# Fourier mixing by halves and mirror images, convolution taps that read PSUM, and an earlier conversion of w_out, in a hybrid Fourier and Mamba-2 block

## The chip, the cores and the metric

The kernel runs on one core of a Trainium2 chip. The metric is the device time of one execution in microseconds (us). The engines are named as in the profile: PE is the matrix engine, PEld its weight load, DVE the vector engine, ACT the scalar engine, POOL the GpSimd engine, and SP the engine that only issues DMA transfers. PE writes its results to PSUM, which PE, DVE and ACT can reach; everything else lies in SBUF.

## The reference, cut to what matters

One layer: 2048 latent tokens of 1024 features and 256 context tokens pass a modulated norm, one input projection, a Fourier part and a bidirectional state-space scan, an output projection, and a feed-forward network. What the change touches is the part between input and output projection:

```python
def conv_rows(u, w, bias, rows, row_len):            # rows of 64 tokens; D_CONV = 7
    up = jnp.pad(u.reshape(b, rows, row_len, ch), ((0, 0), (0, 0), (half, half), (0, 0)))
    out = bias
    for k in range(D_CONV):
        out = out + up[:, :, k:k + row_len, :] * w[:, k]
    return out.reshape(b, L, ch)

def fourier_mix(u):                                  # 256 features = 4 groups of 64; 2048 tokens
    ug = u.reshape(b, L, N_FGROUPS, FGROUP_DIM).astype(jnp.float32)
    yf = jnp.fft.fft2(ug, axes=(1, 3), norm='ortho').real
    return yf.reshape(b, L, F_WIDTH).astype(u.dtype)

def mixer_inputs(h, w_in, conv_w, conv_b, rows, row_len, full):
    p = h @ w_in
    u_f, z, rest = p[..., :F_WIDTH], p[..., F_WIDTH:XBC_OFF], p[..., XBC_OFF:]
    xbc = jax.nn.silu(conv_rows(rest[..., :CONV_DIM], conv_w, conv_b, rows, row_len))
    ...

def mixer_output(u_f, z, xs, y, d_skip, g_ssd, w_out):
    ...
    y = rms_norm(y * jax.nn.silu(z), g_ssd)
    return jnp.concatenate([fourier_mix(u_f), y], axis=-1) @ w_out
```

The Fourier part needs only the real part of a two-dimensional transform of real input. Such a transform has a symmetry: the value at (token frequency l, feature frequency f) is the complex conjugate of that at (-l, -f).

## The kernel before, in words

**Stages.** The first 760 us or so hold the input projection with everything that hangs on it: the convolutions, the step sizes ("dt"), the forward scan, the Fourier part, and the split of weights. After it come the output stage, chunk by chunk, and the feed-forward network. All matmuls of the projection are done in three passes of a 32-bit format (hi x hi, hi x lo, lo x hi), so each weight block is split into `hi` and `lo` (`wparts`, on ACT and on POOL or DVE), and so is w_out (`load_wo`, ACT and DVE).

**Blocks.** The projection is a list `blocks` of 128 output columns each, for three sections of tokens: 0 and 1 are the halves of the latent tokens (1024 each), 2 is the context (256). Kinds: z (gate), u (Fourier input), x, B, C (convolved), and dt. A block of a latent section is 48 matmuls of 512 columns (`project`, 2 halves x 8 x 3), into a PSUM tile "mm" of two banks, of which there are two. A further PSUM pair "y" serves dt, the first Fourier stage and the output stage; two single banks "a" serve transposes, the scan, the second Fourier stage and other small work. Those are all eight banks.

**Convolution.** `conv` copies the finished block from PSUM to a tile `u` (ACT), forms the middle tap with the bias (ACT, from PSUM, into `acc`), and then runs six taps on DVE, each a multiply-add of `u`, shifted, into `acc`. `to_tokens` then transposes the block through PE in two groups of four into "a" banks, and ACT copies these out.

**Fourier.** `fourier_steps` runs once section 1's u blocks are done, for one half of the 256 features after the other (`fb`). For each, the first stage multiplies 16 token groups with the matrix `dft1` (cosines and sines of all 64 feature frequencies, two groups of 64 features side by side, 256 columns); a radix-4 `butterfly` (POOL one subtraction, DVE one addition and six halves and quarters) and complex turns (two ACT copies, two DVE operations each) follow, four times (`j`); then, for four `p`, another butterfly and the second stage: 8 matmuls with constants `kf` that are loaded from memory each time, and one ACT copy into `fo`. So there are 16 butterflies. `fo` is written to memory at the end of each half.

**What sets the order.** PE, DVE, ACT and POOL execute in the order in which the program writes their instructions. That order comes from a planner, `Pace`: each side job (a block's convolution, the Fourier step, the scan, the modulation rows `ada_steps`) is a generator, a chain with a time at which its next step is due; after each matmul step of a block, `pace.due()` issues the steps whose time has come by the planner's own costs (a DVE multiply-add costs 0.06 us + n/960, for instance). `spare()` holds a Fourier step back while the planner believes DVE to be more than 1.2 us behind. `pace.drain(chains)` issues the rest of a chain at once. `finish_block` drains the chains of all earlier blocks but the last before a new one goes on. DMA loads are issued from SP (`dma`), most stores from ACT (`put`); a queue issues in order, and a load that must wait for its buffer holds up those behind it.

**The end of the stage.** At the last block but two the chains of all blocks but z, and the scan, are drained; at the last block the Fourier step, the first chunk's front, and the conversion of the first half of w_out (`late`) are; the conversion of the second half runs beside that last block. `late_steps` starts the first conversion when the Fourier step is done:

```python
        def late_steps():
            fourier_load(pend[0])
            decay_loads(pend[0])
            late.append(pace.start(load_wo(0, "B"), 4.0))
```

The lines that name the operations: in the profile nearly every instruction carries the planner's helper line L140, so groups are told apart by their tiles: `acc<-u,convw,acc` is a tap, `u<-mm` the copy from PSUM, `y<-kc,actB` the first Fourier stage, `a<-kf,gg` the second, `gg` and `actB` the butterflies and turns, `a<-ident,acc` a transpose, `h<-h,a` a step of the scan's state, `dtp` the dt chain, `actB<-wo` a conversion of w_out.

Of the kernel before, what the change touches and what calls it, by code (L numbers as in the profile page):

```python
# [21 lines left out]
P = 128  # L22
# [10 lines left out]
HD = 64  # L33
# [8 lines left out]
def shape_constants():  # L42
# [8 lines left out]
    dft1 = np.zeros((2, HD, 2, 2, HD))  # L51
    f = np.arange(HD)
    ang = 2 * np.pi * ((f[:, None] * f[None, :]) % HD) / HD
# [4 lines left out]
    dft1 = dft1.reshape(P, 4 * HD).astype(np.float32)  # L58
# [10 lines left out]
class Pace:  # L69
# [43 lines left out]
    def drain(self, *chains):  # L113

        self.forced += 1
        for chain in chains:
            while not chain.done:
# [44 lines left out]
def fourier_ssd_block(ctx, tc, a):  # L162
# [87 lines left out]
    kc = cq.tile([P, 2 * P + 24 + 256], F32, name="kc")  # L250
# [152 lines left out]
    hdec = cq.tile([P, NCH + 2, 24], F32, name="hdec")  # L403
    acs_d = [scratch(f"acsd{h}", [8 * 24, P]) for h in range(2)]
# [14 lines left out]
    def project(w, acts, half=None, beside=None):  # L419
        ps = mm()  # L420
# [13 lines left out]
    def dt_section(acts, sec):  # L434
# [3 lines left out]
        ps = pair()  # L438
# [9 lines left out]
        S.copy(sb[:, 0 : nch * P], ps[0:48].rearrange("p a b -> p (a b)")[:, 0 : nch * P])  # L448

# [70 lines left out]
    def conv(ps, n, row, j, res):  # L520
        long = n == HALF
        u = g_.tile([P, n], F32, tag="u" if long else "l_cT", name="u")
        convs.append(u)
        S.copy(u, ps[:, 0:n])
        acc = g_.tile([P, n], F32, tag="acc" if long else "sc", name="acc")
        S.activation(acc, ps[:, 0:n], AF.Identity, bias=convb[:, j : j + 1], scale=convw[:, j, 3:4])
        yield
        ur = u.rearrange("p (r c) -> p r c", c=row)
        ar = acc.rearrange("p (r c) -> p r c", c=row)
        for k in (2, 4, 1, 5, 0, 6):  # L530
# [3 lines left out]
            while convs[0] is not u:  # L534
                yield 0.1
# [3 lines left out]
        convs.pop(0)  # L539
        S.activation(acc, acc, AF.Silu)  # L540
# [15 lines left out]
    def column_block(kind, j, sec, ps):  # L556
# [4 lines left out]
        if kind == "x":  # L561
            yield from conv(ps, n, row, j, res)
            yield from to_tokens(res[0], n, xtok_d[sec], j)
        elif kind == "B":
            yield from conv(ps, n, row, XB + j, res)
# [3 lines left out]
        elif kind == "C":  # L569
            yield from conv(ps, n, row, XB + BB + j, res)  # L570
            put(cT_d[sec][j], res[0])
        elif kind == "z":
            sz = g_.tile([P, HALF], F32, tag="tok", name="sz")
            S.activation(sz, ps, AF.Silu)
            put(szT_d[sec][j], sz)
            last_sz[:] = [sz]
        elif kind == "u":
            uf = g_.tile([P, HALF], F32, tag="tok", name="uf")
            S.copy(uf, ps)
            put(ufT_d[sec][j], uf)  # L580
# [89 lines left out]
    def butterfly(dst, src, pool):  # L670
# [6 lines left out]
        V.tensor_tensor(dst(0), s[:, 0, :], s[:, 1, :], op=ALU.add)  # L677
        V.tensor_tensor(dst(2), s[:, 0, :], s[:, 1, :], op=ALU.subtract)
        re, im = slice(0, P), slice(P, 2 * P)
        V.tensor_tensor(dst(1)[:, re], d[:, 0, re], d[:, 1, im], op=ALU.add)  # L680
        V.tensor_tensor(dst(1)[:, im], d[:, 0, im], d[:, 1, re], op=ALU.subtract)
        V.tensor_tensor(dst(3)[:, re], d[:, 0, re], d[:, 1, im], op=ALU.subtract)
        V.tensor_tensor(dst(3)[:, im], d[:, 0, im], d[:, 1, re], op=ALU.add)
        yield

    def fourier_steps():
        tt = act("B", F32, (P, 4, 4, 256))
        wk = act("B", F32, (P, 4, 4, 256))
        for fb in range(2):
            uf = wk[:, 0:2].rearrange("p a b c -> p (a b c)")  # L690
            for h in range(2):
                dma(uf[:, h * HALF : (h + 1) * HALF], ufT_d[h][fb])
            yield 10.0
            for j in range(4):
                ps = pair()
                for m in range(4):
                    n2 = 4 * m + j
                    T.matmul(ps[:, m // 2, (m % 2) * 256 : (m % 2 + 1) * 256], uf[:, n2 * P : (n2 + 1) * P], dft1,
                             start=True, stop=True)
                va = wk[:, 2]  # L700
                S.copy(va.rearrange("p (a b) c -> p a (b c)", a=2), ps)
                yield
                yield from butterfly(lambda p: tt[:, p, j, :], va, wk[:, 3])
                for ps_ in ((1, 2), (3,)) if j else ():
                    turned = []
                    for i, p in enumerate(ps_):
                        th = -2 * math.pi * j * p / 16
                        xx, tm, tn = tt[:, p, j, :], wk[:, 3, 2 * i, :], wk[:, 3, 2 * i + 1, :]
                        S.activation(tm, xx, AF.Copy, scale=0.0 if j * p == 4 else math.cos(th))
                        S.copy(tn, xx)  # L710
                        turned.append((xx, tm, tn, math.sin(th)))
                    yield from spare()
                    for xx, tm, tn, ci in turned:
                        V.scalar_tensor_tensor(xx[:, 0:P], tn[:, P : 2 * P], -ci, tm[:, 0:P], ALU.mult, ALU.add)
                        V.scalar_tensor_tensor(xx[:, P : 2 * P], tn[:, 0:P], ci, tm[:, P : 2 * P], ALU.mult, ALU.add)
                    yield
            fo = wk[:, 0:2].rearrange("p a b c -> p (a b c)")
            fov = fo.rearrange("p (l q r) -> p r q l", q=4, r=4)
            for p in range(4):
                kf = g_.tile([P, 4, 2, P], F32, tag="xt", name="kf", bufs=4)  # L720
                dma(kf, a["k_f"][:, p])
                gg = g_.tile([P, 4, 256], F32, tag="xt", name="gg", bufs=4)
                yield from butterfly(lambda q: gg[:, q, :], tt[:, p], wk[:, 3])
                yield 0.3
                ps = bank()
                for q in range(4):
                    for i in range(2):
                        T.matmul(ps[:, q * P : (q + 1) * P], gg[:, q, i * P : (i + 1) * P], kf[:, q, i, :],
                                 start=i == 0, stop=i == 1)
                S.copy(fov[:, p], ps.rearrange("p (q l) -> p q l", q=4))  # L730
                yield
            put(fT_d[fb], fo)
# [566 lines left out]
    def load_wo(n, slot):  # L1299

        wo_hi.append(act(slot))
        wo_lo.append(act(slot))
        for kp in range(KD // 2):
            raw = wo_raw.pop(0) if n else wo_load(n, kp)
            for kk in range(2):
# [5 lines left out]
                yield  # L1311
        if n == 0:
            wo_raw.extend(wo_load(1, kp) for kp in range(KD // 2))
# [30 lines left out]
    with tc.manual_schedule(engines=ordered):  # L1344
# [144 lines left out]
        def finish_block(bi, ps):  # L1489
# [6 lines left out]
            chains[bi] = pace.start(column_block(kind, j, sec, ps.rearrange("p a b -> p (a b)")))  # L1496
# [12 lines left out]
        while bi < nblk:  # L1509
            kind, j, sec = blocks[bi]  # L1510
            if kind == "dt":
# [3 lines left out]
                chains[bi] = pace.start(dt_section(acts[sec], sec))  # L1515
# [11 lines left out]
            if bi == first1:  # L1527
                b1 = after(bi, 1)
                want(after(bi, 3))
                pz = [mm(), mm()]  # L1530
# [9 lines left out]
                fnet = pace.start(when(lambda: settled("u", 1), fourier_steps()))  # L1540
                bi += 2
# [397 lines left out]
```

## Time and profile before

| | us |
|---|---|
| median of 3 runs | 2409.01 (2407.45 to 2411.35) |
| profiled execution, its own time | 2409.39 |
| its span | 2407.6 |
| PE busy | 2281.4 (95%) |
| DVE busy | 1669.3 (69%) |
| ACT busy | 1113.6 (46%) |
| POOL busy | 1049.4 (44%) |

The profile is of one execution. A group row gives the engine, the operation, what is written and read, the count, then busy time, mean ns of one, and the idle time of the engine just before with what ended it. A row of the chain of waits gives who waited for whom: total us, times, longest. A timeline row gives start, length, engine, operation, and the number merged. A row of busy time by stage gives the stretch, its length, the busy time (and count) of PE, PEld, DVE, ACT and POOL, the clock granted to PE as a share of full speed, the DMA share and GB/s.

### The profile page before, as it was taken

To read this page: it belongs to the slowest core of one execution; us is meant where nothing else is said; L and a number is where in the kernel's file an instruction comes from. 1 tells how busy PE (TensorE), PEld (TensorE's weight loads), DVE (VectorE), ACT (ScalarE), POOL (GpSimd) and SP (SyncE) were. 2 spreads that over 40 slices of the span, in tenths; PEclk is the share of its full clock that TensorE was granted. 3 is DMA by queue.
4 is the path that set the end of the run, shared out by engine and by line. 5 is a ranking of instruction groups with operands and counts; after the bars stand their busy time and mean duration, and the time that the engine had idled before them with its cause. 6 is when DMAs were issued, how large, how long until landed. Compare 5 with 4: busy or idle time off the path is not lost. (4 is left out here: it accounts for less than half of the span.)

```text
span 2407.6 us, 30176 instructions
## 1 busy us (share of the span) xinstructions
PE 2281.4 (95%) x10861; PEld 1865.9 (77%) x10861; DVE 1669.3 (69%) x2255; ACT 1113.6 (46%) x2017; POOL 1049.4 (44%) x667
## 2 busy tenths in 40 slices
PE   7999798999989999988999999899999999998998
PEld 3887667777778888876788888788888878876786
DVE  3559878588976888887555555855555665778666
ACT  4535453355428677765623333333323335444354
POOL 2121536635552444443454555355554541425512
PEclk9999998999999999998999999999999999999999
DMA  9355435445466888842333333433333373547333
GB/s 310 129 158 156 131 120 186 147 152 177 152 214 226 263 257 252 256 168 90 121 97 110 106 105 105 149 113 97 109 97 102 105 268 117 186 140 262 95 123 118
DMA packets 272580, 377.20 MB, mean 157 GB/s; under 512 B 17111, under 2 KB 190115, under 8 KB 269358
## 3 DMA queue, kind: packets, MB, share of 16 engines
q1 hardware_dynamic: 243062, 344.49, 44.7%
q10 hardware_dynamic: 29368, 30.78, 3.7%
q8 instruction: 86, 1.41, 0.3%
q14 instruction: 64, 0.52, 0.1%
HBM read 280.49 MB, written 94.72 MB: 156 GB/s over the span
## 5 line engine op out<-in xcount | busy, mean ns | idle before, releaser
L140 PE MATMUL b<-wd,hd 128*128 128x512 f32 x1848 | 429.5, 394 | 15.9 <-DVE hd L140 10.8
L140 PEld LDWEIGHTS b<-wd,hd 128*128 128x128 f32 x1848 | 350.1, 190 | 95.1 <-DVE hd L140 13.5
L140 PE MATMUL mm<-slot,wa 128*128 128x512 f32 x1584 | 378.6, 392 | 10.5 <-ACT sg L140 6.6
L140 PEld LDWEIGHTS mm<-slot,wa 128*128 128x128 f32 x1584 | 297.6, 189 | 75.7 <-ACT sg L140 7.4
L140 DVE SCALAR_TENSOR_TENSOR acc<-u,convw,acc 128x992 f32<-128x992 f32 (+5 forms) x228 | 310.5, 1366 | 23.5 <-ACT acc L140 19.1
L140 POOL TENSOR_TENSOR ws<-raw 128x512 f32<-128x512 f32 x88 | 127.4, 1448 | 310.3 <-DMA raw<-in_w_up_dram 131.4
L140 PE MATMUL mm<-actC,wa 128*128 128x512 f32 x984 | 241.5, 394 | 7.4 <-DVE u L140 7.2
L140 PE MATMUL mm<-actB,wa 128*128 128x512 f32 x1020 | 239.4, 390 | 0.0
L140 PE MATMUL mm<-actA,hi 128*128 128x512 f32 x704 | 227.7, 404 | 3.8 <-DVE actA L140 2.7
L140 ACT CAST wa<-ws 128x512 fp32r<-128x512 f32 x176 | 109.2, 621 | 252.9 <-PE mm L140 215.2
L140 PEld LDWEIGHTS mm<-actC,wa 128*128 128x128 f32 x984 | 186.6, 190 | 47.6 <-issue 8.7
L140 PEld LDWEIGHTS mm<-actB,wa 128*128 128x128 f32 x1020 | 191.2, 188 | 39.6
L140 DVE TENSOR_TENSOR wa<-ws,wa 128x512 fp32r<-128x512 f32 x176 | 156.9, 893 | 59.3 <-ACT wa L140 56.3
L140 POOL TENSOR_TENSOR rq_y<-rq_ms,mhalf 128x1 f32<-128x1 f32 (+2 forms) x60 | 43.1, 723 | 288.6 <-DVE rq_ms L140 274.5
L140 DVE TENSOR_TENSOR u<-u,mm 128x512 f32<-128x512 f32 x126 | 86.4, 686 | 116.4 <-PE mm L140 116.4
L140 DVE TENSOR_TENSOR wa<-raw,wa 128x512 fp32r<-128x512 f32 x132 | 118.4, 898 | 65.2 <-ACT wa L140 64.7
L140 ACT CAST wa<-raw 128x512 fp32r<-128x512 f32 x132 | 82.3, 624 | 163.1 <-PE mm L140 147.7
L140 PEld LDWEIGHTS mm<-actA,hi 128*128 128x128 f32 x704 | 130.1, 191 | 33.4 <-issue 3.7
L140 POOL TENSOR_TENSOR adacc<-adacc,adaw 128x1024 f32<-128x1024 f32 x28 | 74.1, 2648 | 181.8 <-ACT adaw L140 169.8
L140 POOL TENSOR_TENSOR lo<-raw,hi 128x1024 fp32r<-128x1024 f32 x34 | 90.2, 2652 | 128.4 <-ACT hi L140 128.4
L140 PE MATMUL mm<-actC,hi 128*128 128x512 f32 (+1 forms) x512 | 144.6, 370 | 0.0
L140 PE MATMUL mm<-actA,lo 128*128 128x512 f32 x352 | 139.2, 396 | 0.6 <-DVE lo L140 0.6
(280 smaller groups left out, 4459.1 us busy)
## 6 DMA issues: line engine op xcount, KB each, us to landing
hraw<-hg SPq DMA_DIRECT2D x70, 512.0 KB, 4.0
raw<-in_w_in_dram SPq DMA_DIRECT2D x54, 512.0 KB, 5.1
ab<-acsd SPq DMA_DIRECT2D x128, 192.0 KB, 4.8
raw<-in_w_gate_dram SPq DMA_DIRECT2D x44, 512.0 KB, 4.6
raw<-in_w_up_dram SPq DMA_DIRECT2D x44, 512.0 KB, 3.8
hg<-hs SPq DMA_DIRECT2D x22, 1024.0 KB, 5.0
adaw<-in_w_ada_dram SPq DMA_DIRECT2D x32, 512.0 KB, 3.8
l_x<-xtok SPq DMA_DIRECT2D x33, 384.0 KB, 4.2
```

Source lines behind the costliest of these rows:

```text
L140: r = issue(out, *args, **kw)
```

## The change

*Fourier.* `dft1` keeps feature frequencies 0 to 31 of each group of 64; the column of frequency 0 has no imaginary part, and its second place carries frequency 32. Both feature halves are done in one pass: 8 butterflies in place of 16. Frequencies 33 to 63 are then filled as mirror images by ACT (reversed copies, negated for the imaginary part), and 0 and 32 by small DVE sums from a saved copy `z0`. The first stage writes to two "a" banks in place of "y". The constants `kf` are loaded once for both halves, into the tile "dtp" or into parts of `tt` that are used up. The result is copied out in 16 pieces and stored by four DMAs at the end.

*Taps.* `conv` no longer copies to `u`; the six taps read PSUM. A PSUM slot is therefore held until the last tap; a function `done` marks that, and `place` hands out slots: "m", "m", "y" in turn (until the last block but two), after `vacate` has issued the work that frees the slot. dt blocks take their slot from the same rotation.

*w_out.* The first half is converted when the Fourier step is done, and its four loads are issued one ahead; at the last block but one that is drained and the second half's four loads are issued (before: both after the Fourier step, drained at the last block).

```diff
-    dft1 = np.zeros((2, HD, 2, 2, HD))
-    f = np.arange(HD)
+    dft1 = np.zeros((2, HD, 2, 2, HD // 2))
+    f = np.arange(HD // 2)
...
+        dft1[g, :, 0, g, 0] = s / 2
+        dft1[g, :, 1, g, 0] = np.cos(np.pi * np.arange(HD)) * s / 2
...
+    held = {"m": [], "y": []}
+    read, places = set(), [0, 3]
+
+    def vacate(tag):
+        b = held[tag].pop(0)
+        pace.drain(chains[b], until=lambda: b in read)
+
+    def place(bi):
+        tag = "y" if places[0] % places[1] == 2 else "m"
+        places[0] += 1
+        if len(held[tag]) == {"m": 2, "y": 1}[tag]:
+            vacate(tag)
+        held[tag].append(bi)
+        return pair() if tag == "y" else mm()
+
-    def project(w, acts, half=None, beside=None):
-        ps = mm()
+    def project(bi, w, acts, half=None, beside=None):
+        ps = place(bi)
...
-    def conv(ps, n, row, j, res):
+    def conv(ps, n, row, j, res, done):
         long = n == HALF
-        u = g_.tile([P, n], F32, tag="u" if long else "l_cT", name="u")
-        convs.append(u)
-        S.copy(u, ps[:, 0:n])
         acc = g_.tile([P, n], F32, tag="acc" if long else "sc", name="acc")
         S.activation(acc, ps[:, 0:n], AF.Identity, bias=convb[:, j : j + 1], scale=convw[:, j, 3:4])
...
-        ur = u.rearrange("p (r c) -> p r c", c=row)
+        ur = ps[:, 0:n].rearrange("p (r c) -> p r c", c=row)
...
         convs.pop(0)
+        done()
...
     def fourier_steps():
         tt = act("B", F32, (P, 4, 4, 256))
-        wk = act("B", F32, (P, 4, 4, 256))
+        wk = act("B", F32, (P, 16, 256))
+        uf = wk.rearrange("p (f a) c -> p f (a c)", f=2)
...
+        for j in range(4):
+            va, sd = (g_.tile([P, 4, 256], F32, tag="xt", name="va", bufs=4) for _ in range(2))
+            ps = [bank(), bank()]
+            for m in range(4):
+                n2 = 4 * m + j
+                for fb in range(2):
+                    T.matmul(ps[m // 2].rearrange("p (m c f e) -> p m c f e", m=2, c=2, f=2)[:, m % 2, :, fb, :],
+                             uf[:, fb, n2 * P : (n2 + 1) * P], dft1, start=True, stop=True)
+            for a_ in range(2):
+                S.copy(va[:, 2 * a_ : 2 * a_ + 2].rearrange("p b c -> p (b c)"), ps[a_])
+            yield
+            yield from butterfly(lambda p: tt[:, p, j, :], va, sd)
...
+        for group_ in ((0,), (2,), (1, 3)):
+            kfs = {}
+            for p in group_:
+                kf = {1: tt[:, 2], 3: tt[:, 1]}.get(p)
+                if kf is None:
+                    kf = g_.tile([P, 4, 2, P], F32, tag="dtp", name="kf", bufs=1)
...
+                yield from butterfly(lambda q: st[p][:, q, :, :, 0:32], tt[:, p], tt[:, 0] if p else wk[:, 8:12],
+                                     lambda t: t.rearrange("p (c g f) -> p c g f", c=2, f=32))
+                dma(kf, a["k_f"][:, p])
+                kfs[p] = kf
+                V.tensor_copy(z0[:, p, 0:4], st[p][:, :, :, :, 0])
...
+            for p in group_:
+                o = st[(4 - p) % 4]
+                for i in range(2):
+                    for qs, qo in ...:
+                        S.activation(st[p][:, qs, i, :, 33:64], o[:, qo, i, :, 31:0:-1], AF.Copy, scale=1.0 - 2.0 * i)
...
+                V.tensor_tensor(st[p][:, :, 0, :, 0], x[:, :, 0], y[:, :, 0], op=ALU.add)
...
+            for p in group_:
+                for fb in range(2):
+                    ps = bank()
...
+                            T.matmul(ps[:, q * P : (q + 1) * P], st[p][:, q, i, 2 * fb : 2 * fb + 2, :].rearrange("p g f -> p (g f)"),
+                                     kfs[p][:, q, i, :], start=i == 0, stop=i == 1)
...
-            late.append(pace.start(load_wo(0, "B"), 4.0))
...
                 fnet = pace.start(when(lambda: settled("u", 1), fourier_steps()))
+                late.append(pace.start(when(lambda: fnet.done, load_wo(0, "B"))))
...
             if bi == plain[-3]:
...
+                places[1] = 1
+                vacate("y")
...
             if bi == plain[-2]:
                 pace.hurry = True
+                pace.drain(*late)
+                wo_raw.extend(wo_load(1, kp) for kp in range(KD // 2))
```

More of the change, by code (lines that the diff above doesn't have):

```diff
@@ L111, in due, with drain @@
                     self.push(chain)
-    def drain(self, *chains):
+    def drain(self, *chains, until=lambda: False):
         self.forced += 1
         for chain in chains:
-            while not chain.done:
+            while not chain.done and not until():
                 issued = self.issued
@@ L533, in conv @@
             o, i = max(0, -off), max(0, off)
-            while convs[0] is not u:
+            while convs[0] is not acc:
                 yield 0.1
@@ L569, in column_block @@
         elif kind == "C":
-            yield from conv(ps, n, row, XB + BB + j, res)
+            yield from conv(ps, n, row, XB + BB + j, res, done)
             put(cT_d[sec][j], res[0])
@@ L668, in spare, with butterfly @@
             yield 0.1
-    def butterfly(dst, src, pool):
+    def butterfly(dst, src, pool, form=lambda t: t):
         s = pool[:, 0:2, :]
@@ L676, in butterfly @@
         yield from spare()
[L677 to L683, printed above, removed]
+        s0, s1, d0, d1 = (form(t) for t in (s[:, 0, :], s[:, 1, :], d[:, 0, :], d[:, 1, :]))
+        half = (lambda t, i: t[:, i]) if len(s0.shape) > 2 else (lambda t, i: t[:, i * P : (i + 1) * P])
+        V.tensor_tensor(dst(0), s0, s1, op=ALU.add)
+        V.tensor_tensor(dst(2), s0, s1, op=ALU.subtract)
+        V.tensor_tensor(half(dst(1), 0), half(d0, 0), half(d1, 1), op=ALU.add)
+        V.tensor_tensor(half(dst(1), 1), half(d0, 1), half(d1, 0), op=ALU.subtract)
+        V.tensor_tensor(half(dst(3), 0), half(d0, 0), half(d1, 1), op=ALU.subtract)
+        V.tensor_tensor(half(dst(3), 1), half(d0, 1), half(d1, 0), op=ALU.add)
         yield
@@ L735, in group @@
+        for fb in range(2):
+            for h in range(2):
+                put(fT_d[fb][:, h * HALF : (h + 1) * HALF], fo[fb][h])
     def group(kind, sec):
@@ L1310, in load_wo @@
                                        ALU.mult, ALU.subtract)
-                yield
-        if n == 0:
-            wo_raw.extend(wo_load(1, kp) for kp in range(KD // 2))
+                yield 1.5
     wo_raw, wo_rest = [], []
@@ L1495, in finish_block @@
             splits[two] = pace.start(split(two, *((V, V) if brief and blocks[two][2] != 2 else (V,) if brief else (G,))))
-            chains[bi] = pace.start(column_block(kind, j, sec, ps.rearrange("p a b -> p (a b)")))
+            chains[bi] = pace.start(column_block(kind, j, sec, ps.rearrange("p a b -> p (a b)"), lambda: read.add(bi)))
         def late_steps():
@@ L1514, in fourier_ssd_block @@
                     pace.drain(scan[2])
-                chains[bi] = pace.start(dt_section(acts[sec], sec))
+                chains[bi] = pace.start(dt_section(acts[sec], sec, place(bi), lambda bi=bi: read.add(bi)))
                 pace.due()
@@ L1529, in fourier_ssd_block @@
                 want(after(bi, 3))
-                pz = [mm(), mm()]
+                pz = [place(bi), place(b1)]
                 pace.drain(splits[b1])
```

106 lines of the change are left out of this document (53 added, 53 removed).

## The prediction

> **What bounds the kernel now.** I read the page first, then busy time by stage, then who TensorE (PE) waits for, then the groups of instructions in the stage that the change touches.
>
> ```profile
> PE 2281.4 (95%) x10861; PEld 1865.9 (77%) x10861; DVE 1669.3 (69%) x2255; ACT 1113.6 (46%) x2017; POOL 1049.4 (44%) x667
> ...
> 100.00:440.00 340.00, 309.38 (x1507) 249.67 (x1506) 257.64 (x270) 149.08 (x196) 129.81 (x58) 0.96 0.50 156
> 440.00:760.00 320.00, 298.43 (x1439) 247.62 (x1437) 263.72 (x324) 153.08 (x213) 149.85 (x69) 0.97 0.52 167
> 760.00:2408.00 1648.00, 1591.22 (x7462) 1312.56 (x7461) 1107.79 (x1587) 762.26 (x1535) 744.88 (x518) 0.99 0.46 150
> ```
>
> The page's first row says PE-bound. The four stage rows (length, then busy time of PE, weight loads, DVE, ACT, POOL, then granted clock) place the change: everything it edits runs between 100 and 760 us, and the 1648 us behind are left as they are. In 100 to 760 PE is idle for 30.6 + 21.6 = 52.2 us and DVE is busy for 257.6 + 263.7 = 521.4 of 660 us (79%). So there are only three sources of gain here: these 52 us, the clock below full speed around them, and PE's own work. Who PE waits for in that stretch:
>
> ```profile
> PE a L140 <- DVE h L140: 11.2, 6, 3.6
> PE a L140 <- DVE dtp L140: 10.3, 2, 6.7
> PE a L140 <- ACT acc L140: 7.1, 5, 2.1
> PE a L140 <- ACT v L140: 6.5, 2, 5.4
> PE a L140 <- DVE gg L140: 5.0, 3, 2.0
> ...
> PE a L140 <- DVE br L140: 1.9, 1, 1.9
> ```
>
> Nearly all of it ends at small matmuls and transposes into the two PSUM banks "a", which PE must do in the written order, and whose input (or whose bank) DVE or ACT releases late. No projection into "mm" waits for its slot. The engine that is behind is DVE.
>
> **The change, part by part.**
>
> *Taps read PSUM.* Removed: the copy of each block out of PSUM. Changed: the source of the six taps of each convolution.
>
> ```profile
> L140 ACT COPY u<-mm 128x1024 f32<-128x1024 f32 x28 | 28.2, 1007 | 1.3 <-PE mm L140 1.3
> L140 DVE SCALAR_TENSOR_TENSOR acc<-u,convw,acc 128x992 f32<-128x992 f32 x56 | 101.8, 1818 | 1.3
> L140 DVE SCALAR_TENSOR_TENSOR acc<-u,convw,acc 128x976 f32<-128x976 f32 x56 | 89.9, 1605 | 1.2
> L140 DVE SCALAR_TENSOR_TENSOR acc<-u,convw,acc 128x1008 f32<-128x1008 f32 x56 | 86.7, 1548 | 19.6 <-ACT acc L140 19.1
> L140 DVE SCALAR_TENSOR_TENSOR acc<-u,convw,acc x228: 381/1250/3489, 100.6 to 714.3; 128x1008 f32<-128x1008 f32 x28, 128x992 f32<-128x992 f32 x28, 128x976 f32<-128x976 f32 x28, 128x255 f32<-128x255 f32 x10
> ...
> 281.34 2.51 DVE L140 SCALAR_TENSOR_TENSOR acc<-u,convw,acc 128x1008 f32<-128x1008 f32 x1
> ...
> 281.31 1.48 POOL L140 TENSOR_TENSOR xd<-l_x,scs 128x768 f32<-128x768 f32 x1 [0.66 <-PE a L140]
> ...
> L140 DVE TENSOR_TENSOR h<-h,a x34: 486/542/555, 272.6 to 741.9; 128x384 f32<-128x384 f32 x34
> L140 DVE SCALAR_TENSOR_TENSOR o<-mm,rq_y,o 128x1024 f32<-128x1024 f32 x15 | 19.3, 1283 | 12.9 <-POOL rq_y L140 12.9
> L140 DVE SCALAR_TENSOR_TENSOR o<-o,rq_y,gmix 128x1024 f32<-128x1024 f32 x15 | 19.1, 1272 | 0.7 <-POOL rq_y L140 0.7
> ```
>
> The key reading: a long tap's mean is 1.55 to 1.82 us although the median over all taps, short ones too, is 1.25, with a maximum of 3.49. The long ones are those that meet a POOL instruction: the tap at 281.34 ends 1.06 us after POOL's 1.48 us are over, so it ran, in effect, after it. A DVE add that takes one operand from PSUM and one from SBUF shows nothing of this: the 34 state adds h<-h,a, in the same stretch and beside the same POOL work, lie between 486 and 555 ns. So a tap with its source in PSUM should take its undisturbed time each time. The same instruction form at 1024 elements takes 1283 ns with a PSUM source and 1272 ns with SBUF sources. I take 1.25 us per long tap; the bounds are 1.24 (the undisturbed tap) and, if POOL still blocks it, the present mean (101.8 + 89.9 + 86.7) / 168 = 1.66. DVE saves 278.4 - 168 x 1.25 = 68 us; the short taps I leave alone. ACT saves 28.2 us of long copies.
>
> [...]
>
> What the change adds here is a longer hold: a PSUM slot is now freed after the last tap, not after two ACT reads. In this run the block whose ACT read starts at 603.75 has its last tap end at 629.57, 25.8 us later.
>
> ```profile
> 603.75 1.21 ACT L140 ACTIVATE acc<-mm,vcol,convw 128x1024 f32<-128x1024 f32 x1
> ...
> 628.35 1.22 DVE L140 SCALAR_TENSOR_TENSOR acc<-u,convw,acc 128x976 f32<-128x976 f32 x1
> ...
> 228.86 0.62 PE L140 MATMUL mm<-actA,hi 128*128 128x512 f32 x2
> 229.54 0.62 PE L140 MATMUL mm<-actA,hi 128*128 128x512 f32 x2
> ```
>
> With "y" joined to the rotation a slot comes round after three blocks. Three matmuls take 0.68 us (229.54 - 228.86), so a block of 48 takes 10.9 us, and two blocks between are 21.8 us plus whatever the transposes and Fourier matmuls add; that is about equal to the worst hold seen with slow taps, and beyond a hold with taps of 1.25 us, which is some 8 us of taps and 1.2 us of ACT when DVE is free. Also, the written order already puts a block's transposes, which need its last tap, ahead of the block after next. I cost the slot wait at nothing; DVE's shorter queue is the cover, and without it each microsecond over 22 is one of PE.
>
> *Fourier on half of the features, both feature blocks at once.*
>
> ```profile
> L140 PE MATMUL y<-kc,actB 128*128 128x256 f32 x64 | 15.2, 380 | 0.0
> 541.71 1.95 PE L140 MATMUL a<-kf,gg 128*128 128x128 f32 x16
> ...
> L140 POOL TENSOR_TENSOR actB<-actB 128x512 f32<-128x512 f32 x16 | 30.9, 1929 | 22.6 <-PE a L140 8.3 <-DVE gg L140 5.5 <-DVE actB L140 4.8
> L140 DVE TENSOR_TENSOR gg<-actB 128x256 f32<-128x256 f32 x16 | 18.5, 1196 | 0.0
> L140 DVE TENSOR_TENSOR actB<-actB 128x512 f32<-128x512 f32 x16 | 17.4, 1090 | 1.0 <-ACT actB L140 1.0
> L140 DVE TENSOR_TENSOR actB<-actB 128x256 f32<-128x256 f32 x16 | 16.2, 1051 | 0.0
> L140 DVE SCALAR_TENSOR_TENSOR actB<-actB 128x128 f32<-128x128 f32 x36 | 15.5, 484 | 0.0
> L140 DVE TENSOR_TENSOR gg<-actB 128x128 f32<-128x128 f32 x32 | 7.1, 278 | 0.0
> L140 ACT COPY actB<-a 128x512 f32<-128x512 f32 x8 | 8.5, 1064 | 43.2 <-PE a L140 43.2
> L140 ACT COPY tok<-a 128x512 f32<-128x512 f32 x40 | 23.2, 588 | 44.6 <-PE a L140 44.6
> ```
>
> PE, first stage: 64 instructions stay 64, but each moves 128 columns instead of 256. At the second stage's rate (16 of 128 columns in 1.95 us) they take 64 x 0.122 = 7.8 us in place of 15.2 (a lower bound for PE's share, since they run back to back with projections): 7.4 us saved. The second stage keeps its 128. Butterflies go from 16 to 8 and turns from 36 instructions to 18. POOL saves 8 x 1.93 = 15.4 us. DVE saves half of 18.5 + 17.4 + 16.2 + 15.5, or 34 us; the halved 128-wide adds (32 fewer, with the like group on actB, at about 0.28 us) pay for the 21 new tiny ones (edge columns). ACT gains ten mirror copies of at most 496 elements, between 0.59 us (contiguous copy of 512) and 1.06 us (the present scattered one), about 7 us, and splits its scattered output copies in two; it loses half the turns' copies. That is even, on an engine busy for 46%. These mirrors, however, stand between butterfly and matmul: a chain of POOL, DVE, ACT, DVE before each of three groups, where now it is POOL and DVE. I raise PE's wait for this stage from 5.0 to 9 us (bounds: 5.0 as now; 3 groups and 4 first-stage steps x 4 us = 28). The first stage also leaves its own PSUM pair for the two "a" banks, so transposes behind it wait for ACT's 0.59 us copies; that is inside the 9.
>
> *Queues.* SP's loads wait in order.
>
> ```profile
> SPq L211 <- POOL lo L140: 75.4, 15, 10.7
> ...
> L140 DVE SCALAR_TENSOR_TENSOR actB<-wo,vcol,actB x6: 742/750/752, 726.5 to 744.2; 128x512 fp32r<-128x512 f32 x6
> ```
>
> The second-stage constants are loaded four times instead of eight, but into one "dtp" buffer (the second load waits for PE's use of the first) and into spent parts of tt; behind them in SP stand the w_in loads of line 211, which already wait up to 10.7 us for a buffer without any PE wait on a weight in the table above, since they are two blocks ahead. On ACT's queue the Fourier results leave in four issues at the end instead of two. I cost both at nothing; without the two blocks of lead a load wait would fall on PE in full.
>
> *w_out sooner.* Eight conversions (0.75 us each on DVE, as much on ACT) and their four loads move from 724 to 744 us to just after the Fourier step, where DVE is fuller, and the second half's four loads to the block before the last but one. PE shows no wait for them now: no gain; 6 us of DVE if its cover were gone, and that is less than the 34 freed.
>
> **The sum.** DVE's busy time in 100 to 760 falls from 521 to about 521 - 68 - 34 = 419 us, its free time from 139 to 241. Of PE's 52.2 us I then expect: backlog waits (h, acc, v and seven smaller ones, 52.2 - 10.3 - 5.0 - 1.9 = 35.0) down to a third, 11.7; the dt chain (some twenty dependent small DVE operations, queued between taps) from 10.3 to 6; Fourier 5.0 to 9; br stays 1.9. That is 28.6, a gain of 23.6. Behind a long wait the clock is low for a while:
>
> ```profile
> 484.73 1.17 PE L140 MATMUL a<-dtp,kc 128*128 128x96 f32 x4 [6.68 <-DVE dtp L140]
> 486.13 1.31 PE L140 MATMUL mm<-actC,hi 128*128 128x512 f32 x2
> 487.24 0.63 PE L140 MATMUL mm<-actC,lo 128*128 128x512 f32 x1
> ```
>
> After the wait of 6.68 us two projection matmuls take 1.11 us (487.24 - 486.13) where two thirds of 0.68, 0.45, are usual: about half speed or less. Where that lasts 4 us it loses 2. For some five such places I count 10 us (an estimate; the stage rows' clock of 0.96 and 0.97 of 660 us is 23 us short of full speed, part of it inside the waits) and take back 5. Sum: 23.6 + 5 + 7.4 = 36.0. The profiled execution took 2409.39 us (span 2407.6), 0.4 above the median 2409.01; 2409.4 - 36.0 gives 2373.4, and against the median 2373.
>
> **The rivals.**
> (1) The waits come from the written order, not from DVE's lag: the planner that writes it charges taps 1.09 us and now issues sooner whatever is cheaper. Then the 52 us stay and only PE's work falls: 2409 - 7 = 2402. For it: waits such as br and dt are chains of dependent steps. Against: DVE h and ACT acc lead the table, both behind taps.
> (2) The Fourier step's longer chain and its shared banks hold PE at the upper bound of 28 us, not 9: 2373 + 19, and 5 more of low clock, 2397.
> (3) Slower: a tap from PSUM, in rows of 62 or so elements, costs as much as a tap behind POOL now. At 2.4 us (the 2.51 us row is near) the 168 taps take 403 instead of 278 us; less 34, DVE is at 612 of 660 us. Half of the 91 us that it gains falling on PE, through held slots: 2409 + 46 - 7 = 2448. It turns from gain to loss for DVE where a tap passes (278 + 34) / 168 = 1.86 us. Against it: 1283 against 1272 ns. [...]
>
> **How the numbers follow.** Forecast 0.68, its own range 2352 (all backlog waits gone, 11.7, all low clock back, 5, Fourier at 5.0, 4) to 2390; order 0.13; Fourier chain 0.10; slower 0.09. The range 2351 to 2405 leaves out the slower rival and thin tails. About 0.2% (5 us) is what a measurement of this kernel tells from no change: faster takes the forecast, most of the second rival and two thirds of the first, 0.84; same the rest of these, 0.07; slower 0.09.
>
> **What would show it.** Right: long taps all at 1.2 to 1.3 us with no long ones beside POOL; DVE near 420 us in the stage; no PE wait on "mm" for DVE; the first stage at about 8 us; waits on h and acc mostly gone; the stage's end (now 753 to 760) near 720. Wrong: PE waiting into "mm" or "y" for DVE acc, taps above 1.86 us, PE waits above 3 us ahead of each second-stage group, or SP's load waits showing up as PE waits on weights.

## The result and the profile after

The changed kernel takes 2374.8 us (median of 4 runs, 2373.2 to 2376.4) against 2409.05 (4 runs of the kernel before, 2407.45 to 2411.35): a ratio of 0.9858 [0.9845, 0.987]. The forecast was 2373. The size was right; its composition was partly not.

The page and the busy time by stage of the kernel after (length, then PE, PEld, DVE, ACT, POOL, clock, DMA share, GB/s):

```profile
PE 2261.2 (95%) x10861; PEld 1854.2 (78%) x10861; DVE 1557.1 (66%) x2202; ACT 1079.6 (45%) x1978; POOL 999.8 (42%) x659
...
100.00:440.00 340.00, 319.08 (x1584) 260.85 (x1584) 219.79 (x276) 136.37 (x175) 118.93 (x63) 0.96 0.53 162
440.00:760.00 320.00, 302.50 (x1535) 253.00 (x1534) 216.69 (x322) 157.67 (x263) 122.23 (x65) 0.99 0.58 182
760.00:2375.00 1615.00, 1557.47 (x7284) 1284.09 (x7282) 1079.42 (x1528) 736.71 (x1468) 733.73 (x510) 0.99 0.45 147
```

DVE's load in 100 to 760 fell from 521.4 to 436.5 us, but these windows now hold some output stage, which began sooner. So I cut at a mark that is the same work in every kernel: the transpose of `mr` (`a<-ident,mr`), PE's first instruction of the output stage. Before, the two stretches read

```profile
100.00:752.70 652.70, 600.50 (x2884) 490.84 (x2882) 517.24 (x588) 296.34 (x400) 275.50 (x124) 0.97 0.51 162
752.70:2407.60 1654.90, 1598.52 (x7522) 1319.01 (x7521) 1111.91 (x1594) 768.08 (x1544) 749.05 (x521) 0.99 0.46 150
```

and after

```profile
100.00:721.50 621.50, 583.08 (x2879) 480.35 (x2878) 407.20 (x536) 264.84 (x366) 226.90 (x117) 0.98 0.54 167
721.50:2374.60 1653.10, 1595.97 (x7522) 1317.58 (x7521) 1108.70 (x1590) 765.91 (x1539) 748.00 (x521) 0.99 0.46 150
```

The stage ends 31.2 us sooner: 17.4 us of it are less PE busy time, 13.8 less PE idle time (52.2 to 38.4). Behind the mark 1.8 us more are gained. DVE did 110 us less work in the stage. Who PE waits for in 100 to 760 after the change (total, times, longest):

```profile
PE a L143 <- ACT acc L143: 8.6, 4, 4.0
PE mm L143 <- DVE acc L143: 8.4, 2, 6.4
PE a L143 <- ACT v L143: 6.3, 1, 6.3
PE a L143 <- DVE h L143: 4.5, 2, 2.4
PE a L143 <- DVE dtp L143: 4.1, 1, 4.1
PE a L143 <- issue: 2.6, 2, 1.8
PE a L143 <- ACT hdec L143: 1.7, 1, 1.7
PE a L143 <- DVE br L143: 0.7, 1, 0.7
```

`DVE gg` (5.0) is gone, `h` fell from 11.2 to 4.5, `dtp` from 10.3 to 4.1. `ACT v` stayed (6.5, now 6.3), `ACT acc` even rose, and the second row is new: PE waits to write into "mm" until the taps have read it. The groups of instructions after:

```profile
L143 DVE SCALAR_TENSOR_TENSOR acc<-mm,convw,acc 128x1008 f32<-128x1008 f32 x38 | 47.9, 1261 | 16.8 <-ACT acc L143 16.5
L143 DVE SCALAR_TENSOR_TENSOR acc<-mm,convw,acc 128x976 f32<-128x976 f32 x38 | 46.8, 1232 | 0.9
L143 DVE SCALAR_TENSOR_TENSOR acc<-y,convw,acc x72: 473/1238/1270, 128.0 to 669.5; 128x1008 f32<-128x1008 f32 x18, 128x992 f32<-128x992 f32 x18, 128x976 f32<-128x976 f32 x18, 128x255 f32<-128x255 f32 x6
...
L143 PE MATMUL a<-kc,actB 128*128 128x128 f32 x64 | 8.2, 278 | 1.7 <-ACT hdec L143 1.7
L143 PE MATMUL a<-actB 128*128 128x128 f32 x64 | 7.9, 276 | 0.8 <-issue 0.8
L143 PE MATMUL a<-kf,actB 128*128 128x128 f32 x64 | 7.8, 275 | 0.0
...
L143 POOL TENSOR_TENSOR lo<-raw,hi 128x1024 fp32r<-128x1024 f32 x31 | 74.7, 2411 | 195.8 <-ACT hi L143 192.2 <-DMA adaw<-in_w_ada_dram 3.7
```

The long taps of a form take 1.23 to 1.26 us on average, and the longest of the last group 1.27, where the longest was 3.49. The first Fourier stage takes 8.2 us instead of 15.2. The second, unchanged in count and form, is the surprise: it takes 7.9 + 7.8 = 15.7 us, and before, in the same view, in PE's timeline, and in busy time by windows (the clock is the last but two),

```profile
L140 PE MATMUL a<-kf,gg 128*128 128x128 f32 x128 | 20.0, 315 | 12.3 <-DVE gg L140 5.0 <-DVE h L140 4.6 <-issue 1.6
```
```profile
531.05 2.93 PE L140 MATMUL a<-kf,gg 128*128 128x128 f32 x12 [1.95 <-DVE gg L140]
```
```profile
531.00:534.00 3.00, 2.95 (x13) 2.95 (x14) 2.96 (x5) 0.00 (x0) 2.15 (x1) 0.50 0.63 188
```

it took 20.0, with 12.3 us of waits ahead of its matmuls. Twelve of them behind one such wait take 2.93 us; sixteen without one, shown in the prediction, take 1.95. The clock granted in those 3 us, right behind the wait of 1.95 us, is 0.50; from 524 to 529, up to the wait, it is 1.00 in the same view.

The new wait, in the timelines of PE and of DVE:

```profile
225.79 0.80 PE L143 MATMUL mm<-actA,hi 128*128 128x512 f32 x1 [6.37 <-DVE acc L143]
```
```profile
207.55 1.51 DVE L143 SCALAR_TENSOR_TENSOR acc<-mm,convw,acc 128x255 f32<-128x255 f32 x3
...
218.06 7.67 DVE L143 SCALAR_TENSOR_TENSOR acc<-mm,convw,acc 128x1008 f32<-128x1008 f32 x6
```

The last long block of a section is followed by two context blocks of 256 columns. The slot that the long block holds comes round after these two, and DVE starts the long block's six taps only at 218.06; they end at 225.73, and PE goes on at 225.79.

### The profile page after: what moved, and what is told of

Read it like the earlier page. It is cut to its first block, busy times and chain, and to the rows that moved or that the text cites. A ratio compares the mean times of both kernels' runs of the same rounds, so it can differ in the third digit from the quotient of the medians.

```text
span 2374.6 us, 30049 instructions
## 1 busy us (share of the span) xinstructions
PE 2261.2 (95%) x10861; PEld 1854.2 (78%) x10861; DVE 1557.1 (66%) x2202; ACT 1079.6 (45%) x1978; POOL 999.8 (42%) x659
## 5 line engine op out<-in xcount | busy, mean ns | idle before, releaser
L143 PE MATMUL b<-wd,hd 128*128 128x512 f32 x1848 | 429.2, 394 | 16.1 <-DVE hd L143 10.8
L143 PE MATMUL mm<-actA,hi 128*128 128x512 f32 x512 | 165.9, 405 | 9.6 <-DVE acc L143 6.4
L143 DVE SCALAR_TENSOR_TENSOR acc<-mm,convw,acc 128x1008 f32<-128x1008 f32 (+3 forms) x156 | 161.9, 1040 | 19.5 <-ACT acc L143 16.5
L143 POOL TENSOR_TENSOR lo<-raw,hi 128x1024 fp32r<-128x1024 f32 x34 | 81.8, 2407 | 204.4 <-ACT hi L143 200.8
L143 POOL TENSOR_TENSOR adacc<-adacc,adaw 128x1024 f32<-128x1024 f32 x28 | 68.3, 2439 | 136.8 <-ACT adaw L143 136.8
L143 DVE TENSOR_TENSOR hd<-hraw,hd 128x512 fp32r<-128x512 f32 x154 | 117.3, 764 | 8.3 <-ACT hd L143 8.3
L143 PEld LDWEIGHTS mm<-actA,hi 128*128 128x128 f32 x512 | 95.1, 192 | 33.2 <-DVE acc L143 6.6
L143 ACT ACTIVATE ab<-ab,lda 128x128 f32<-128x128 f32 x384 | 118.8, 391 | 0.4 <-ACT sz L143 0.4
```

What stands on the lines that cost most here:

```text
L143: r = issue(out, *args, **kw)
```

## The experiments

Ratios are to the kernel before on the same chip. The theory was that of the prediction: a PSUM source frees the taps from POOL, the Fourier part gives DVE a little more, and w_out does nothing. The main rival was the written order: that the planner's new order makes the gain, not the time of a tap.

**1. The source of the taps, in the same written order.** In the changed kernel, ACT copies each block to `u` again, outside the planner's accounts, and the taps read `u`.

```diff
+        u = g_.tile([P, n], F32, tag="u" if long else "l_cT", name="u")
+        nc.scalar.copy(u, ps[:, 0:n])
...
-        ur = ps[:, 0:n].rearrange("p (r c) -> p r c", c=row)
+        ur = u.rearrange("p (r c) -> p r c", c=row)
```

> The changed kernel with every instruction in its written place, but each block is copied to SBUF again by ACT and the six taps read that copy; the copy is not charged to the planner, and the PSUM slot is still held to the last tap. Theory of DVE's lag (POOL blocks taps with two SBUF operands): long taps go back to a mean of 1.5 to 1.7 us with some above 2.3, DVE is 50 to 70 us busier in 100 to 740 us, PE's waits grow by 15 to 40 us, and the time is 2392 to 2420 us, against 2374.8. Theory of the written order (waits come from where PE's small matmuls stand, not from DVE's pace): within 4 us of 2375, whatever the taps take.

Measured: 2411.77 us, ratio 1.0014 [1.0005, 1.0022]. PSUM's last reader is here ACT, so only the written order keeps the slots to the last tap. Its groups, and PE's waits in 100 to 760:

```profile
L143 DVE SCALAR_TENSOR_TENSOR acc<-u,convw,acc 128x976 f32<-128x976 f32 x56 | 101.7, 1816 | 1.3
L143 DVE SCALAR_TENSOR_TENSOR acc<-u,convw,acc 128x992 f32<-128x992 f32 x56 | 93.4, 1667 | 1.4
L143 DVE SCALAR_TENSOR_TENSOR acc<-u,convw,acc 128x1008 f32<-128x1008 f32 x56 | 82.8, 1478 | 25.1 <-ACT acc L143 24.6
```
```profile
PE a L143 <- ACT acc L143: 19.5, 9, 6.1
PE a L143 <- DVE h L143: 12.2, 4, 8.4
PE a L143 <- ACT v L143: 11.7, 2, 6.8
```

The long taps are back at 1.48 to 1.82 us, the backlog waits at 43 us, and the whole gain is gone although the order is that of the faster kernel. So the order by itself makes no gain: that rival falls. How much of the 37 us the taps are worth outside this order is another question; experiment 5 bears on it.

**2. The same copy, not read.** The first two lines of the diff above, without the third: it prices ACT's 28 long copies.

> As the last one, but the taps read PSUM and nothing reads the copy: only ACT's 28 us of long copies come back. If the gain is the taps' source, 2375 to 2379 us and long taps at 1.25 us. If a good part of the gain is ACT's relief, 2385 us or more, with PE waiting longer for ACT acc and ACT v.

Measured: 2380.49 us, ratio 0.9877 [0.9862, 0.9892]: 5.7 us above the changed kernel by the medians, a little more than expected, though the two intervals overlap. So of the 37 us between experiment 1 and the changed kernel, the source of the taps alone is 2411.8 - 2380.5 = 31 in this written order, on the same chip; the rest goes with ACT's copies.

**3. Only the taps and slots.** The kernel before with the new `conv`, `place` and `vacate`; Fourier in two passes as before (its first stage in two "a" banks, since "y" is in the rotation) and w_out as before.

```diff
         butterfly, fourier_steps, dft1, load_wo      # as before the change
-                ps = pair()
+                ps = [bank(), bank()]                # first Fourier stage
```

> The kernel before with one part of the change: taps read PSUM and the slots rotate over m, m and y. Fourier as before, in two passes, except that its first stage uses the two a banks since y is in the rotation; w_out as before. DVE's lag: it loses two thirds of the relief at most (68 of 102 us of DVE stay), so 2385 to 2396 us. Written order: PE's work is as before, 2405 to 2411 us.

Measured: 2397.41 us, ratio 0.9948 [0.9936, 0.9961], just above the range that I had expected. The stretches up to the mark and behind it (cut at 726.0, the mark is at 726.2):

```profile
100.00:726.00 626.00, 590.70 (x2876) 485.50 (x2874) 429.84 (x569) 257.60 (x353) 237.69 (x124) 0.98 0.53 165
726.00:2398.30 1672.30, 1600.14 (x7523) 1320.25 (x7521) 1120.98 (x1607) 777.09 (x1558) 748.22 (x521) 0.98 0.46 150
```

The stage ends 26.5 us sooner, but 17.2 us are given back behind it (from the mark itself, 1672.1 against 1654.9). The timelines of PE and ACT there:

```profile
743.97 0.80 PE L141 MATMUL mm<-actB,yh 128*128 128x512 f32 x1 [13.56 <-ACT yh L141]
```
```profile
738.92 1.33 ACT L141 ACTIVATE actC<-wo,ones 128x512 fp32r<-128x512 f32 x2 [6.55 <-DMA wo<-in_w_out_dram]
...
743.53 0.39 ACT L141 CAST yh<-off 128x256 fp32r<-128x256 f32 x1
```

PE waits 13.6 us for one cast of 0.39 us, which stands on ACT behind conversions of w_out, whose loads came late. It looked as if converting w_out sooner were what saves this; experiment 4 asks.

**4. Taps and w_out, Fourier as before.** Experiment 3 with the new `load_wo` and its new places.

> The taps part as in the first study (2397.4 us), now with w_out converted sooner too; Fourier still in two passes. There the stage ended 26.5 us earlier than before, and 14 us were given back right behind it, where PE waited 13.6 us for the split of the Fourier result behind ACT's conversion of w_out, whose load had come late. If the late w_out is what gave the gain back: 2383 to 2388 us and that wait gone. If it is the Fourier step's own late end (two passes end where they did): the wait moves ahead of the last block but one, and 2393 to 2402 us.

Measured: 2403.39 us, ratio 0.9967 [0.9954, 0.9979], just above both ranges: no faster than experiment 3, and by the medians 6 us slower, though the two intervals just overlap. The wait for `yh` is gone, and PE waits at other places of the same end (PE's timeline):

```profile
709.57 5.42 PE L141 MATMUL a<-kf,gg 128*128 128x128 f32 x32 [4.10 <-DVE gg L141]
...
753.27 1.62 PE L141 MATMUL a<-l_h,l_cT 128*128 128x192 f32 x4 [7.59 <-DVE dg L141]
```

So a late w_out was not the bottom of it: with two Fourier passes the end of the stage is crowded, and moving one piece shifts the wait. The second wait is a load's (DVE's timeline: `yg`, from which `dg` follows, waits for `l_sz`):

```profile
749.85 0.96 DVE L141 TENSOR_TENSOR yg<-y,l_sz 128x768 f32<-128x768 f32 x1 [8.16 <-DMA l_sz<-szT]
```

**5. Only the Fourier part.** The kernel before with the new Fourier step; the taps read the copy `u` as before, PSUM is free after ACT's reads, "y" stays with dt, w_out is as before.

```diff
-    read, places = set(), [0, 3]
+    read, places = set(), [0, 1]                      # "m" slots only
...
+        u = g_.tile([P, n], F32, tag="u" if long else "l_cT", name="u")
+        S.copy(u, ps[:, 0:n])
...
+        done()                                        # behind ACT's reads, not the last tap
```

> The kernel before with the other part: Fourier on half of the features in one pass; taps read the SBUF copy, PSUM is free after ACT's reads, y is kept for dt, w_out as before. PE's first stage falls by 7 us and DVE's work by 34 us, taps stay at a mean near 1.6 us. DVE's lag: 2388 to 2398 us. Written order: 2402 us, PE's own work alone. If its longer chain held PE, 2400 to 2409 us.

Measured: 2383.38 us, ratio 0.9893 [0.9879, 0.9906]: better than any theory's range. Its stretch to the mark, and a tap:

```profile
100.00:730.20 630.20, 591.65 (x2882) 485.63 (x2880) 483.23 (x538) 292.73 (x401) 261.93 (x116) 0.97 0.53 164
```
```profile
L143 DVE SCALAR_TENSOR_TENSOR acc<-u,convw,acc 128x976 f32<-128x976 f32 x56 | 96.3, 1719 | 1.2
```

DVE has 517.2 - 483.2 = 34.0 us less, the taps are still slow, and PE's idle time is 38.6 us, as low as with the whole change. In PE's waits, `dtp` fell from 10.3 to 4.3 us, and `gg`, 5.0 before, is replaced by 1.9 for `actB` and 1.2 for `fo`. That is 13.6 us less idle time and 8.9 less busy time, with taps that still meet POOL. Whether DVE's relief, PE's shorter work or the order that the planner wrote for it ends these waits wasn't separated.

This kernel also corrects the reading of experiment 1. Both have the new Fourier step and slow taps, on the same chip, and this one is 28 us faster. Its slots come free after ACT's reads, its order was planned for the copy, and w_out is as before; experiment 1 keeps an order that was written for fast taps. So most of the 37 us there are what slow taps cost in that order. Beside the Fourier part and an order of its own, the taps part adds about 11 us: 2383.4 against 2372.6 in experiment 6, by the medians.

**6. All but the earlier w_out.** The changed kernel with `load_wo` and its places as before.

> The changed kernel with w_out converted as before: the first half after the Fourier step and the decay loads, drained at the last block, the second half's loads behind it. By the prediction this part is worth nothing, since no wait on a w_out conversion stands in the profile before: 2373 to 2377 us. If the earlier conversion carries part of the gain, 2380 us or more, with a PE wait at the last block or right behind it.

Measured: 2372.62 us, ratio 0.9842 [0.9828, 0.9855], beside 0.9858 [0.9845, 0.987]: w_out sooner is worth nothing that can be told here. In the profiled executions the stage even ends 5.3 us sooner without it (mark at 716.2), and 1.0 us is lost behind the mark. The run also closes the sum: taps alone 0.9948 times Fourier alone 0.9893 is 0.9842, the same as both.

**7. The order of blocks and the planner's prices.** Three kernels ask what is left in the 38 us. The first moves an x block in between the two context blocks that follow the last long B block, to mend the 6.4 us wait; the second charges DVE and PE about what the trace shows; the third does both.

```diff
-    blocks += c_[8:]
+    blocks += c_[8:9]
     x_ = group("x", 0)
-    blocks += x_[:5] + [("dt", 0, 0)] + x_[5:] + group("C", 0)
+    blocks += x_[:1] + c_[9:] + x_[1:5] + [("dt", 0, 0)] + x_[5:] + group("C", 0)
```
```diff
-                cost = max(n, 64) * (4 if fp32 else 1) / 2400
+                cost = max(n, 64) * (4 if fp32 else 1) / 2260
...
-                cost = 0.06 + n / (1920 if op in ("tensor_scalar", "tensor_copy") else 960)
+                cost = 0.18 + n / (1920 if op in ("tensor_scalar", "tensor_copy") else 960)
```

Order alone:

> The changed kernel with one entry of the list of blocks moved: the last context x block goes behind the first x block of section 0, so that no long block is followed by two short ones. In the changed kernel PE waits 6.37 us at 219 us for a slot that is held by such a block's taps. If that wait is only the slot's hold against two short blocks, it goes with the low clock behind it: 2364 to 2370 us and no PE wait on mm for DVE acc above 1 us there. If DVE is simply behind at that point, the wait turns up at a transpose instead: 2372 to 2378 us.

Measured: 2373.01 us, 0.9845 [0.9831, 0.9858], not clear of the changed kernel. The wait is mended, another takes its place (PE's waits in 100 to 760; they were 8.4 and 8.6):

```profile
PE a L143 <- ACT acc L143: 12.9, 6, 4.0
...
PE mm L143 <- DVE acc L143: 3.0, 1, 3.0
```

Prices alone:

> The changed kernel with two of the planner's costs nearer to the trace: a DVE instruction 0.18 us + n/960 in place of 0.06 (a tap 1.21 us, measured 1.25), a PE column 1/2260 us in place of 1/2400 (measured 0.227 us for 512). Only the written order changes. If what is left of the waits comes from steps that the planner issues too soon for DVE, 2362 to 2371 us; if it comes from chains of dependent steps, 2371 to 2380 us; the order can also turn out worse, up to 2385 us.

Measured: 2373.05 us, 0.9841 [0.9828, 0.9855]: the same again.

Both:

> Both of the last two edits. If they act on different waits, the sum of their gains: 2355 to 2366 us. If not, as the better of the two.

Measured: 2355.85 us, 0.9771 [0.9758, 0.9785]: faster than both kernels, by far more than the two alone add up to. Its waits and its stages:

```profile
PE mm L143 <- DVE acc L143: 6.3, 4, 2.9
PE a L143 <- ACT acc L143: 6.1, 6, 1.7
```
```profile
100.00:440.00 340.00, 324.57 (x1638) 266.15 (x1638) 222.37 (x296) 143.65 (x184) 119.62 (x64) 0.99 0.53 164
440.00:760.00 320.00, 311.97 (x1610) 260.66 (x1608) 230.37 (x340) 166.84 (x293) 124.83 (x70) 1.00 0.63 196
```

The many waits that remain are short (the longest into "mm" 2.9 us, not 6.4) and the clock is at 0.99 and 1.00.

**8. The same edits on the kernel before.** Both diffs of experiment 7, without the change.

> The kernel before with only the two edits of the written order (the moved context block, and the planner's costs of a DVE instruction and a PE column), which gave 19 us on the changed kernel. Written order as a cause of its own: 2385 to 2398 us. DVE's lag: taps are still blocked by POOL and real taps take 1.66 us against 1.21 planned, so the order can't mend it: 2402 to 2412 us.

Measured: 2417.58 us, 1.0026 [1.0017, 1.0035]: slower than the kernel before, and above both ranges. The loss isn't in the stage: the mark comes at 747.8 instead of 752.7, and PE's idle time up to it is 45.8 us instead of 52.2, although the taps are slow (1808 ns for the 992-wide ones). It lies behind the mark, 1669.0 us instead of 1654.9, where PE meets the wait of experiment 3 again (PE's timeline):

```profile
761.41 0.79 PE L140 MATMUL mm<-actB,yh 128*128 128x512 f32 x1 [9.39 <-ACT yh L140]
```

In ACT's timeline the cast of `yh` stands behind conversions of w_out, and those of the second half waited 4.33 us for their load. So a stage that ends sooner by order alone runs into a late w_out too; the same edits with an earlier w_out weren't run.

**9. Is it the nearer price or one lucky order?** The combination once more, with 0.22 and 2240 in place of 0.18 and 2260.

> The fastest so far (2355.9 us) with the planner's costs moved a little further the same way: 0.22 us + n/960 for DVE (a tap 1.25 us, as measured) and 1/2240 us for a PE column. If nearer costs are the cause of its gain: 2350 to 2360 us. If that order was only a lucky draw: anywhere in 2360 to 2380 us.

Measured: 2365.08 us, 0.981 [0.9797, 0.9823], inside the range that was given to a lucky draw. It is still 9.7 us better than the changed kernel, but 9.2 of the 19 us that experiment 7's best had gained hang on the particular order. More than half of these is one wait that the best doesn't have (PE's waits in 100 to 760):

```profile
PE a L143 <- DMA l_cT<-cT: 5.5, 1, 5.5
```

**10. The best kernel with w_out as before.**

> The fastest so far with w_out converted as in the kernel before. In the changed kernel that made no difference that its interval shows (2372.6 against 2374.8). If w_out sooner is worth nothing, within 4 us of 2356; if the later place is better as such, 2350 to 2354 us; if the end of the stage now comes so early that a late w_out holds PE, 2360 us or more.

Measured: 2364.76 us, 0.9809 [0.9795, 0.9822]: 8.9 us slower than with w_out sooner, although its stage ends as early (mark at 699.9 against 701.5). The loss lies behind the mark, where one wait of PE leads to DVE and from there to a load:

```profile
713.87 1.62 PE L143 MATMUL a<-l_h,l_cT 128*128 128x192 f32 x4 [6.34 <-DVE dg L143]
```
```profile
710.45 0.96 DVE L143 TENSOR_TENSOR yg<-y,l_sz 128x768 f32<-128x768 f32 x1 [8.05 <-DMA l_sz<-szT]
```
```profile
697.18 0.37 SPq L1351 DMA_DIRECT2D wo<-in_w_out_dram  x1
702.18 2.04 SPq L1031 DMA_DIRECT2D ab<-acsd  x3
704.31 0.39 SPq L1019 DMA_DIRECT2D l_sz<-szT  x1
```

The third view is SP's timeline. The load of `l_sz` is issued at 704.31, behind the last load of w_out (697.18) and three others. With w_out sooner, in experiment 7's best, it leaves at 694.97, 6.5 us before the mark (SP's timeline there):

```profile
694.97 0.36 SPq L1019 DMA_DIRECT2D l_sz<-szT  x1
```

Experiment 4 lost its 7.6 us to a late `l_sz` too. Whether w_out's own loads or the three `ab` loads ahead of it hold it up wasn't separated.

The accounts side by side, from the traces (mark, PE's idle time from 100 us to it, the time behind it):

| kernel | mark | PE idle | behind | span |
|---|---|---|---|---|
| before | 752.7 | 52.2 | 1654.9 | 2407.6 |
| after | 721.5 | 38.4 | 1653.1 | 2374.6 |
| 1, taps from the copy | 758.5 | 61.6 | 1652.3 | 2410.8 |
| 3, only taps | 726.2 | 35.3 | 1672.1 | 2398.3 |
| 4, taps and w_out | 736.7 | 42.5 | 1665.6 | 2402.3 |
| 5, only Fourier | 730.2 | 38.6 | 1651.0 | 2381.2 |
| 7, order and prices | 701.5 | 23.3 | 1652.7 | 2354.2 |
| 10, that, w_out as before | 699.9 | 21.2 | 1665.3 | 2365.2 |

## Why the prediction was right, and where it was not

The total, point by point. The prediction's sum was 36.0 us; the two profiled spans differ by 33.0, the medians by 34.3.

**Taps: right.** 1.25 us was taken, 1.23 to 1.26 came; none is slow beside POOL. Experiment 1 shows that the source does it. DVE's fall in the stage was forecast as 68 + 34 = 102 us, and came as 110; experiment 5 shows the 34 by itself (34.0).

**Backlog waits: mis-sized.** The step "backlog waits 35.0 down to a third, 11.7" failed. What is left of these kinds in the table after is acc 8.6, v 6.3, h 4.5, issue 2.6 and two rows under 0.7: 22.9 us, about two thirds. DVE's relief doesn't end waits that the written order makes: `v` and `acc` stayed with DVE busy 66% of the stage instead of 79%, and the best kernel brings `acc`, `v` and `h` from 19.4 to 10.8 with the same DVE work, by order and prices alone. That is the order rival's truth: it was wrong on the gain, and right on a part of what was left.

**Slot hold: wrong.** "I cost the slot wait at nothing" came out at 8.4 us. The working took two long blocks between two uses of a slot, 21.8 us; the list has a place where the two between are context blocks, and there the slot comes round in the time of two short ones, while DVE starts the six taps late. The prediction named this row as a sign of the losing case; it came, but only at two places, and the forecast's sign didn't turn on it.

**dt chain and Fourier waits: the second too pessimistic.** dt was put at 6 and is 4.1. Fourier was put at 9, and is 2.2 (`hdec` 1.7, `fo` 0.5): the mirrors' chain, three times POOL, DVE, ACT, DVE, lies beside other work. Experiment 5 shows what I had underrated: I gave Fourier a third of DVE's relief, and alone it takes 26 us off, more than twice the 12 of the taps alone. The taps' 12 are what the crowded end of experiment 3 leaves of 26.5. So the prediction had the weights the wrong way round: it gave the taps two thirds of DVE's relief, and beside the Fourier part they add about 11 us.

**PE's own work: mis-sized the other way.** First stage 7.4 forecast, 7.0 by the group rows (15.2 to 8.2). "Take back 5" for the low clock was too little: PE's busy time to the mark fell by 17.4, so 10.4 is left beside the first stage. Of it the second Fourier stage is 4.3 (20.0 to 15.7); for the rest there is only the granted clock, 0.98 instead of 0.97 to the mark. That is about 6 us of 620, the 4.3 among them, so some 4 us of less PE work have no cause shown. The three misses nearly cancel: waits 9.8 us worse than forecast (38.4 against 28.6), PE's work 5.0 better, and 1.8 came from behind the mark, so the span fell 3.0 us less than forecast. That the total came this close is in part luck.

**w_out sooner: right here, for a reason that can end.** No gain at a stage end near 720 (experiment 6), 8.9 us at one near 700 (experiment 10). A cost that is hidden today can be uncovered by the next improvement.

**Queues: right for this kernel.** No wait of PE on a weight appeared. But the orders of experiments 4, 9 and 10 each lose 5.5 to 7.6 us of PE to one late load.

What stays open: why the nearer prices and the moved block gain 19 us together and next to nothing alone. Experiment 9 puts about half of it down to one particular order; the other half has no cause shown. Why ACT's copies of experiment 2, on an engine busy for less than half of the stage, should cost PE the 5.7 us of the medians is open too.

## What to carry to other kernels

When an engine looks overloaded, read the spread of one instruction's duration before its count: a mean of 1.8 us over a median of 1.25 said that something beside the instruction itself made some of them slow, and changing where the operand lies took that away without removing a DVE instruction. When a part of a change is priced by taking it out again, ask whether the order that is left was written for it: here the same slow taps cost 37 us in an order written for fast ones, and about 11 beside an order of their own. When a buffer is held longer, don't check the hold against the usual block but against the shortest run of blocks that brings the slot round. And where a planner writes the order, expect part of a gain to be left in waits that its prices make, and price its candidates by several orders, since one order can be worth 9 us by itself.

## What the runs showed of the hardware

In this kernel a tap with a PSUM source, a DVE multiply-add, takes the same time beside POOL as without it. By a count in the trace, the 48 long taps that lie beside POOL instructions for over 90% of their length take 1216 to 1270 ns after the change, and the 81 with POOL quiet 1221 to 1268. Before, with an SBUF source, the 27 long taps beside POOL took 1230 to 3383 ns, 14 of them over 2280, and the 88 with POOL quiet 1219 to 1270. The difference is what a source in PSUM buys here.

POOL gains as well: its `lo<-raw,hi` takes 2411 ns after, and in the same view before

```profile
L140 POOL TENSOR_TENSOR lo<-raw,hi 128x1024 fp32r<-128x1024 f32 x31 | 83.1, 2681 | 118.8 <-ACT hi L140 118.8
```

so the taps' source in SBUF cost both engines time: the same view gives 2423 ns in experiment 3, where the taps read PSUM, and 2692 in experiment 5, where they read the copy. And a wait can cost more than its length: the 128 second-stage Fourier matmuls took 4.3 us more (20.0 against 15.7) when 12.3 us of waits lay among them, and behind a wait of 1.95 us, with four matmuls ahead of it and a granted clock of 1.00 from 524 on, the clock was 0.50 for 3 us. Not each wait of this length does it: after the change PE waits 2.37 us until 269.47, and the granted clock is 1.00 in the 5 us behind. So a wait of 2 us can be worth more than its length, as at 531 us before, and the clock in the trace has to say which one is.
